# Four of eight token blocks by gathered experts, two of them begun in the front

## The chip, the core and the metric

One core of one Trainium2 chip runs the program. The metric is device time in microseconds (us): the median over runs, lower is better. A core has TensorE (PE, matrix products; its weight loads are listed as PEld), VectorE (DVE), ScalarE (ACT), GpSimd (POOL), SyncE (SP, which here only issues transfers) and 16 DMA engines. Each engine works its instructions off in the order in which the program gives them.

## What is computed

A transformer block on 1,024 tokens of 1,024 channels: latent attention and a gated recurrence side by side, a projection, and then a mixture of 16,384 single-vector experts. The change concerns the mixture:

```
q = (h2 @ w_query) -> 8 heads x 2 halves of 128;  s = q . sub_keys   # 128 scores per half
per head: top 16 of each half, then top 16 of the 256 sums -> 128 experts per token
u = expert_u[idx]; v = expert_v[idx]                                 # 1024 numbers each
act = gelu(h2 . u);  y = sum over 128 experts of softmax(best) * act * v;  x += gate2 * y
```

## The kernel before

The **front** does all up to the experts' choice, in two halves of 512 tokens (part 0, part 1): attention in 32 units, `merge_a`, `lru`, `merge_b`, `ffn_in` (output projection, norm, queries and scores). Matrices there are split into a high and a low fp32r part (`split`, `weight`: ACT casts, DVE subtracts) and multiplied in three products (`lin`, 24 matmuls per 1,024 rows).

The 1,024 tokens are eight blocks of 128. A **dense** block has all 16,384 experts computed and weighted by a table G that holds the chosen ones' weights and zeros elsewhere. A **gathered** block (`GATHER`) has only its chosen 128 rows per token fetched: `gather_u` issues 128 indirect transfers on GpSimd's queue, one expert row for each of the 128 tokens (512 KB), and VectorE multiplies each with h2 and sums it (`g_u`, one reduce); `gather_v` fetches 128 times 512 KB of `expert_v`, and TensorE adds four of them at a time into `g_y`. Before, blocks 0 to 4 are dense and 5 to 7 gathered.

`route` makes the final choice for a block from its top-16 lists; `table` makes G for a dense block in 32 steps, four tokens each: a one-hot row `oneB` (VectorE, one instruction of 512 columns), `oneA` (VectorE, four of 128), four matmuls into `ps_G`, two copies to `gs` on ACT, and now and then a store to `d_G`. These steps, and those of the gathers, wait in a list, `self.steps`, and `pump(n)` takes n of them out at fixed places of the main program, whose order they then share. What is left over after part 1 is taken out in one go (the **tail** of the front).

The **dense stage** runs over 128 groups of 128 experts (i). `first(i)` multiplies the dense tokens with `uT[i]` (`ps_A`, with gelu to `a`); `weigh(i)` multiplies with G and splits (`w`); `second` adds the products with `expert_v` for NGRP groups at once in PSUM (`ps_y`), and VectorE adds that to sums in SBUF (`yac`). After each product of `first` (24 matmuls) and each block of tokens of `second` stands one pump of the gather steps (a point), at a rate that spends them by 91% of these points (`RATE`); only the routes of the gathered blocks go faster, two steps a point. The loads of `uT` and `expert_v` go through two buffers, `raw`, on SP's queue, one serving `uT` and one `expert_v`; the split `v` has NGRP + 1 buffers.

The longest path in the program is set by this written order; nothing is rearranged at run time.

Of the kernel before, what the change touches and what calls it, by code (L numbers as in the profile page):

```python
# [9 lines left out]
F32 = mybir.dt.float32  # L10
# [69 lines left out]
class Builder:  # L80
    def __init__(self, ctx, tc, I, out, dbg=None, stop=None):
# [8 lines left out]
        self.rate = dict(unit=(1, 2), ma=3, lru=6, mb=2, z=4, q=2)  # L90
# [40 lines left out]
    def pump(self, n):  # L131

        for _ in range(min(n, len(self.steps))):
            self.steps.pop(0)()
# [226 lines left out]
    def head(self, p):  # L361
# [67 lines left out]
        def up(u):  # L429

            n = (768, 768, 1024)[u]
            raw = fp.tile([128, n], F32, tag="raw", bufs=3, name="wupraw")
# [53 lines left out]
    def attention(self, p):  # L486
# [7 lines left out]
        vn = self.b8([128, 4, 512], F32, "vn")  # L494
        rq = fp.tile([128, 4, 8], F32, tag="rq", bufs=2, name="rq")
# [40 lines left out]
        def keys(h, blocks):  # L536
            t = heads.setdefault(h, {})
            if 0 in blocks:
# [3 lines left out]
                if p:  # L542
                    nc.sync.dma_start(t["k"][:, 0:512], self.d_k[h])
                    if h % 2 == 0:
                        t["vold"] = fp.tile([128, 4, 128], F32, tag="vold", bufs=2, name="vold")
                        nc.sync.dma_start(t["vold"], self.d_v[:, :, h * 64:h * 64 + 128])
                    else:
                        t["vold"] = heads[h - 1]["vold"]
# [10 lines left out]
        def values(h, i, P):  # L559
# [16 lines left out]
            def mix():  # L576
                for kb in range(n):
                    v = t["vold"][:, kb, :] if kb < p * 4 else vn[:, kb - p * 4, hp * 128:(hp + 1) * 128]
# [96 lines left out]
    def lru(self, p, hs, gb):  # L675
# [7 lines left out]
        def gate(g):  # L683
            t = grp[g] = [fp.tile([128, G, 512], F32, tag="t4", bufs=9, name=nm) for nm in ("ge", "rr", "uu", "bx")]
            for m in range(G):
                wt = self.weight(I["w_in"][8 + g * G + m], 1024)
                ps = self.psum([128, 512], "ps_g")
                self.lin(ps, wt, hs)
                nc.scalar.activation(t[0][:, m, :], ps, AF.Gelu_apprx_tanh)
# [52 lines left out]
        for g in range(8 // G):  # L742
            gate(g)
            for m in range(G):
                conv(g * G + m)
            if g:
                scan(g - 1)
            self.pump(self.rate["lru"])
        for m in range(G):
            gates(8 - G + m)  # L750
            gb(m)
        scan(8 // G - 1)
        self.pump(self.rate["lru"])
# [4 lines left out]
    def merge_a(self, p, hs, attn):  # L758
# [3 lines left out]
        for m in range(8):  # L762
# [9 lines left out]
            self.pump(self.rate["ma"])  # L772
# [15 lines left out]
    def merge_b(self, p, gb, rec, yf):  # L788
        nc, I, fp = self.nc, self.I, self.fp
        for m in range(8):  # L790
# [9 lines left out]
            self.pump(self.rate["mb"])  # L800
# [12 lines left out]
    def ffn_in(self, p, ys):  # L813
# [12 lines left out]
        for cq in range(4):  # L826
# [13 lines left out]
            self.pump(self.rate["z"])  # L840
# [6 lines left out]
        self.normalise(xs, lambda i: fp.tile([128, 1024], F32, tag="raw", bufs=3, name="junk"))  # L847
# [45 lines left out]
        def score(c):  # L893
            qT = qTs.pop(c)
            sk = fp.tile([128, 128], F32, tag="sk", bufs=4, name="sk")
# [9 lines left out]

        late = [i for i in range(4) if p * 4 + i in GATHER]
        for i in range(4):
            if i not in late:
                self.routes[p * 4 + i] = st[:, i], it[:, i]
        soon = [] if 0 in late else self.route(p * 4)[0]  # L910
        self.soon[p * 4] = soon
        for c in range(17):
# [9 lines left out]
            self.pump(self.rate["q"])  # L922
            while len(self.ahead) > max(ahead * (AHEAD - 1 - c) // AHEAD, 0):
                self.ahead.pop(0)()
        if late:
            a, b = late[0], late[-1] + 1
            d = self.d_st[p * 4 + a:p * 4 + b].rearrange("t p k c -> p k t c")
            nc.gpsimd.dma_start(d[:, 0], st[:, a:b].rearrange("p i a b -> p i (a b)"))
            nc.gpsimd.dma_start(d[:, 1], it[:, a:b].rearrange("p i a b -> p i (a b)").bitcast(F32))
# [12 lines left out]
    def route(self, tb):  # L942

        nc = self.nc
        late = tb in GATHER
# [20 lines left out]
        def start():  # L966

            if late:
                sit = self.gv([128, 2, 256], F32, "sit")
                self.after(nc.sync.dma_start(sit, self.d_st[tb]), self.mark)  # L970
# [42 lines left out]
        def pick(w):  # L1013

            eq = new("raw", [128, 128, 16], BF16, "eq", 3)
# [8 lines left out]
        def end():  # L1024
# [6 lines left out]
            if tb in GATHER:  # L1031
                g = self.blocks[tb]
                for n, dt in (("w", F32), ("ei", I32), ("eT", I32)):
                    g[n] = self.gp.tile([128, 128], dt, tag="g_" + n, bufs=3, name="g_" + n)
# [20 lines left out]


    def gather_u(self, g):

        nc, gp, I = self.nc, self.gp, self.I
        us = {}  # L1060

# [350 lines left out]
```

## Time and profile before

| what | value |
|---|---|
| median of 3 runs | 3806.28 us (3798.11 to 3807.5) |
| profiled execution | 3811.1 us, of which the span of the profile is 3809.3 us |
| front, part 1: first unit of attention to last query | 728 to 1640 us |
| front's tail | 1640 to 1720 us |
| dense stage, first matmul to last | 1720 to 3772 us |
| TensorE busy | 3427.5 us, 90% of the span; mean granted clock 0.95 |

A window row of the profile gives, for a stretch of the span, the busy time of each engine (and its instructions), then the clock granted to TensorE as a share of full speed, the mean busy share of the 16 DMA engines, and the GB/s moved. A timeline row gives start, duration, engine, line, operation, what is written and read, a count of merged instructions, and in brackets the idle time before and what ended it.

### The profile page before, as it was taken

Reading aid. Unit: us, or ns where it says so; the run is one execution under the profiler, and the core shown is the slowest. Engines: PE = TensorE matmul, PEld = TensorE weight load, DVE = VectorE, ACT = ScalarE, POOL = GpSimd, SP = SyncE. Lnnn points to the kernel's source line nnn. Section 1 sums busy time; section 2 is a strip of 40 time slices with the busy share of each in tenths; the row PEclk is TensorE's granted clock in tenths of the full one; section 3 lists DMA queues with packets and bytes.
Section 4 is the critical chain, followed back from the end, with each engine's and each line's share of the span. In section 5 each row is a group of like instructions: output and inputs, shape, how many; then the busy total and the mean of one; then the engine's idle time right before and its main releaser. Section 6 shows DMA issues by size and latency. Waiting matters only on the chain. (4 is left out here: it accounts for less than half of the span.)

```text
span 3809.3 us, 50002 instructions
## 1 busy us (share of the span) xinstructions
PE 3427.5 (90%) x18805; PEld 2810.2 (74%) x18805; DVE 2543.8 (67%) x5976; ACT 1271.9 (33%) x2054; POOL 938.1 (25%) x798
## 2 busy tenths in 40 slices
PE   6899989689988966569988999999999999999997
PEld 4577778467876855558977887787788777877786
DVE  5535548986677565588978876677767766744455
ACT  4437443377466332234222222221222222221121
POOL 0000013000000000000144445555555555444400
PEclk8899999799999987779999999999999999999998
DMA  7422443121423331145588899999989999998932
GB/s 306 151 83 90 139 147 119 47 98 42 149 83 119 133 113 54 58 163 151 182 272 276 279 315 326 335 342 342 330 308 335 335 338 324 311 306 310 316 103 92
DMA packets 382521, 792.48 MB, mean 208 GB/s; under 512 B 188660, under 2 KB 209140, under 8 KB 373448
## 3 DMA queue, kind: packets, MB, share of 16 engines
q1 hardware_dynamic: 271464, 385.80, 31.0%
q0 software_dynamic: 110816, 403.49, 29.3%
q8 instruction: 148, 2.42, 0.3%
q14 instruction: 93, 0.76, 0.1%
HBM read 720.23 MB, written 68.96 MB: 207 GB/s over the span
## 5 line engine op out<-in xcount | busy, mean ns | idle before, releaser
L669 PE MATMUL ps_A<-dh,u 128*128 128x320 f32 x2048 | 609.7, 311 | 5.2 <-DVE yac L1267 5.2
L1070 POOL DMA_INDIRECT g_u<-in_expert_u,g_ei x384 | 453.7, 1181 | 620.3 <-DMA raw<-in_uT 218.1
L670 PE MATMUL ps_A<-dh,u 128*128 128x320 f32 x2048 | 605.9, 309 | 0.0
L1076 DVE CUSTOM_DVE_ANT_0 g_u<-g_u,g_h 128x1024 f32<-128x1024 f32 x384 | 465.5, 1222 | 191.8 <-DMA g_u<-in_expert_u,g_ei 190.6
L669 PE MATMUL ps_y<-v,w 128*128 128x512 f32 x1280 | 515.7, 403 | 49.5 <-DVE yac L1267 40.4
L1100 POOL DMA_INDIRECT g_v<-in_expert_v,g_eT x384 | 433.3, 1128 | 459.0 <-PE g_y L1114 131.6
L670 PE MATMUL ps_y<-v,w 128*128 128x512 f32 x1280 | 504.4, 394 | 0.1
L1267 DVE TENSOR_TENSOR yac<-yac,ps_y 128x512 f32<-128x512 f32 x630 | 414.1, 682 | 95.5 <-PE ps_y L672 94.2
L98 ACT CAST v<-raw 128x1024 fp32r<-128x1024 f32 x128 | 134.5, 1050 | 890.1 <-PE ps_y L672 543.4
L669 PEld LDWEIGHTS ps_A<-dh,u 128*128 128x128 f32 x2048 | 385.3, 188 | 38.2 <-issue 20.1
L672 PE MATMUL ps_y<-v,w 128*128 128x512 f32 x1280 | 402.9, 394 | 2.2 <-DVE w L99 0.7
L670 PEld LDWEIGHTS ps_A<-dh,u 128*128 128x128 f32 x2048 | 385.5, 188 | 1.8
L1169 PE MATMUL ps_G<-oneA,oneB 128*128 128x128 f32 x1280 | 226.0, 329 | 160.1 <-DVE oneA L1165 148.3
L669 PEld LDWEIGHTS ps_y<-v,w 128*128 128x128 f32 x1280 | 242.4, 189 | 168.7 <-DVE yac L1267 64.6
L672 PE MATMUL ps_A<-dh,u 128*128 128x320 f32 x2048 | 343.2, 310 | 0.0
L1169 PEld LDWEIGHTS ps_G<-oneA,oneB 128*128 128x128 f32 x1280 | 202.0, 230 | 191.4 <-issue 123.2
L672 PEld LDWEIGHTS ps_A<-dh,u 128*128 128x128 f32 x2048 | 312.4, 189 | 0.0
L99 DVE TENSOR_TENSOR v<-raw,v 128x1024 fp32r<-128x1024 f32 x128 | 156.3, 1221 | 217.5 <-ACT v L98 217.5
L672 PEld LDWEIGHTS ps_y<-v,w 128*128 128x128 f32 x1280 | 242.3, 189 | 62.2 <-DVE w L99 10.0
L670 PEld LDWEIGHTS ps_y<-v,w 128*128 128x128 f32 x1280 | 242.6, 190 | 46.2 <-DVE v L99 0.5
L99 DVE TENSOR_TENSOR whl<-wraw,whl 128x1024 fp32r<-128x1024 f32 (+2 forms) x136 | 155.2, 1145 | 151.1 <-ACT whl L98 151.0
L1172 ACT COPY gs<-ps_G 128x256 f32<-128x256 f32 x320 | 167.6, 641 | 219.5 <-PE ps_G L1169 193.9
(348 smaller groups left out, 5797.2 us busy)
## 6 DMA issues: line engine op xcount, KB each, us to landing
raw<-in_uT SPq DMA_DIRECT2D x128, 512.0 KB
raw<-in_expert_v SPq DMA_DIRECT2D x128, 512.0 KB
d_G<-gs SPq DMA_DIRECT2D x40, 1024.0 KB
Gt<-d_G SPq DMA_DIRECT2D x64, 640.0 KB
wraw<-in_w_in SPq DMA_DIRECT2D x64, 512.0 KB
wada<-in_w_ada SPq DMA_DIRECT2D x32, 512.0 KB
wraw<-in_w_query SPq DMA_DIRECT2D x32, 512.0 KB
x<-in_x SPq DMA_DIRECT2D x16, 512.0 KB
```

Of the source, the lines that this page charges most:

```text
L98: self.nc.scalar.copy(hi, src)
L99: (eng or self.nc.vector).tensor_tensor(lo, src, b32(hi), op=ALU.subtract)
L669: nc.tensor.matmul(ps, lh, rh, start=(n == 0), stop=False)
L670: nc.tensor.matmul(ps, lh, rl, start=False, stop=False)
L672: st = nc.tensor.matmul(ps, ll, rh, start=False, stop=(n == len(terms) - 1))
L1070: st = nc.gpsimd.indirect_dma_start(out=u[:], out_offset=None, in_=I["expert_u"], in_offset=bass.IndirectOffsetOnAxis(ap=g["ei"][:, s:s + ...
L1076: nc.vector.tensor_tensor_reduce(out=u, in0=u, in1=g["h2"], scale=1.0, scalar=0.0, op0=ALU.mult, op1=ALU.add, accum_out=g["act"][:, s:s + 1])
L1100: st = nc.gpsimd.indirect_dma_start(out=v[:], out_offset=None, in_=I["expert_v"], in_offset=bass.IndirectOffsetOnAxis(ap=g["eT"][:, t:t + ...
L1169: nc.tensor.matmul(ps[:, m, :], B[:, m, :], A[:, m, :], start=True, stop=True)
L1172: nc.scalar.copy(t["st"][m][:, :, k:k + 4].rearrange("p i t -> p t i"), ps[:, :, m * 64:(m + 1) * 64])
L1267: nc.vector.tensor_tensor(yac[tb][:, ds], yac[tb][:, ds], ps, op=ALU.add)
```

## The change

Blocks 0, 1, 6 and 7 are gathered, and 2 to 5 dense, so the dense matmuls have 512 tokens and no longer 640. The u rows of blocks 0 and 1 are fetched and reduced in part 1 of the front, through two buffers (`GUF`), between the table steps of blocks 2 and 3; their v rows, and all of blocks 6 and 7, stay in the dense stage. `oneA` goes to GpSimd. `second` adds four groups (NGRP 4, with four `v` buffers, not five), G is stored in pieces of 16 tokens, the front's `raw` has two buffers for three, the top-16 lists of three of each four blocks go through DRAM on SP's queue, and gate2 is loaded for each block at the end.

```diff
-GATHER = (5, 6, 7)
+GATHER = (0, 1, 6, 7)
+SOONER = tuple(b for b in GATHER if b < 4)
+LATER = tuple(b for b in GATHER if b >= 4)
...
-GC = 32
-NGRP = 2
-GU, GV, WB = 4, 8, 3
+GC = 16
+NGRP = 4
+GU, GV, WB = 4, 8, 4
+GUF = 2
...
-        self.rate = dict(unit=(1, 2), ma=3, lru=6, mb=2, z=4, q=2)
+        self.rate = dict(unit=(1, 3.6), w=(1.5, 3.6), z=(4, 8), q=(2, 4))
+        self.credit = 0.0
...
-        raw = self.fp.tile([128, cols], F32, tag="raw", bufs=3, name="wraw")
+        raw = self.fp.tile([128, cols], F32, tag="raw", bufs=2, name="wraw")
...
     def pump(self, n):
 
+        self.credit += n
+        n = int(self.credit + 1e-6)
+        self.credit -= n
...
-            self.pump(self.rate["ma"])
+            self.pump(1.5 * self.rate["w"][p])
...
-        if late:
-            a, b = late[0], late[-1] + 1
-            d = self.d_st[p * 4 + a:p * 4 + b].rearrange("t p k c -> p k t c")
-            nc.gpsimd.dma_start(d[:, 0], st[:, a:b].rearrange("p i a b -> p i (a b)"))
...
+        d = self.d_st[p * 4 + 1:p * 4 + 4].rearrange("t p k c -> p k t c")
+        nc.sync.dma_start(d[:, 0], st[:, 1:4].rearrange("p i a b -> p i (a b)"))
...
+    def after_part(self, p):
+
+        tbs = [tb for tb in range(p * 4, p * 4 + 4) if tb not in LATER]
+        rt = {tb: self.soon.pop(tb) if tb in self.soon else self.routed(tb) for tb in tbs}
+        side = [rt[tb] + self.table(tb) for tb in tbs if tb in DENSE]
+        for tb in tbs:
+            if tb in SOONER:
+                self.steps += rt[tb] + self.merge(self.gather_u(self.blocks[tb]), side.pop(0))
+        self.steps += sum(side, [])
...
+        sooner = g["tb"] in SOONER
+        gp, GUN = (self.fp, GUF) if sooner else (self.gp, GU)
...
-                u = us[s] = gp.tile([128, 1024], F32, tag="gu", bufs=GU, name="g_u")
+                u = us[s] = gp.tile([128, 1024], F32, tag="gu", bufs=GUN, name="g_u")
...
-            s -= GU - 1
+            s -= GUN - 1
...
-        nc.vector.tensor_tensor(gr, y, self.gate2, op=ALU.mult)
+        self.bcast_row(gr, 5)
+        nc.vector.tensor_tensor(gr, y, gr, op=ALU.mult)
...
-                nc.vector.tensor_scalar(A[:, m, :], iota, ch[:, 0, n:n + 1], ch[:, 2, n:n + 1], op0=ALU.is_equal,
+                nc.gpsimd.tensor_scalar(A[:, m, :], iota, ch[:, 0, n:n + 1], ch[:, 2, n:n + 1], op0=ALU.is_equal,
...
-        points = (128 * 2 + len(groups) * NB) * RATE
+        points = (128 * -(-TD // 512) + len(groups) * NB) * RATE
...
-                Vs[i] = load(I["expert_v"][i * 128:(i + 1) * 128, :], da, "v", NGRP + 1)
+                Vs[i] = load(I["expert_v"][i * 128:(i + 1) * 128, :], da, "v", NGRP)
...
-            us = [self.gather_u(self.blocks[tb]) for tb in GATHER]
+            us = [self.gather_u(self.blocks[tb]) for tb in LATER]
             vs = [self.gather_v(self.blocks[tb]) for tb in GATHER]
-            for b in range(len(GATHER) + 1):
-                self.steps += self.merge(us[b] if b < len(GATHER) else [], vs[b - 1] if b else idle * IDLE[1])
+            for n, v in enumerate(vs):
+                self.steps += self.merge(us[n] if n < len(us) else [], v)
```

Where instructions move is seen on three engines. First VectorE in `merge_a` of part 1, where `whl` is the low part of a weight that TensorE waits for, and `yf` the gated product; before:

```order
L771 TENSOR_TENSOR yf<-ps_pa,sg 128x512
L1165 TENSOR_SCALAR oneA<-cst,ch 128x128
L1161 TENSOR_TENSOR oneB<-cst,ch 128x512
L1165 TENSOR_SCALAR oneA<-cst,ch 128x128 x4
L99 TENSOR_TENSOR whl<-wraw,whl 128x1024
L99 TENSOR_TENSOR whl<-wraw,whl 128x512
```

The same place with the change (g_u is a reduce over a fetched row, g_act the read-out of its sum):

```order
L777 TENSOR_TENSOR yf<-ps_pa,sg 128x512
L103 TENSOR_TENSOR whl<-wraw,whl 128x1024
L103 TENSOR_TENSOR whl<-wraw,whl 128x512
L1102 ISA g_u,g_act<-g_u,g_h_6060 128x1024
L1102 ISA g_act 128x1
L1102 ISA g_u,g_act<-g_u,g_h_6060 128x1024
L1102 ISA g_act 128x1
L1189 TENSOR_TENSOR oneB<-cst,ch 128x512 x2
```

So reduces that wait for a transfer now stand between the weight splits, and the `oneA` rows are gone from this queue. Counted over the whole order, the 256 reduces of part 1 stand 69 in the attention units, 35 in `merge_a`, 45 in `lru`, 35 in `merge_b`, 32 in `ffn_in` ahead of the queries and 40 among the queries. Of the one-hot steps, 126 stood in part 1 and 34 in the tail; with the change 64 and 64.

Second GpSimd's queue in part 1. Before, it held two stores of the top-16 lists between part 0 and the dense stage:

```order
L347 TENSOR_TENSOR hT<-nfull,hT 128x512 x2
L99 TENSOR_TENSOR whl<-wraw,whl 128x1024 x12
L928 DMA d_st<-st 128x3x256
L929 DMA d_st<-it 128x3x256
L1070 DMA g_u<-in_expert_u,g_ei 128x1024 x128
```

With the change (a piece of it):

```order
L1193 TENSOR_SCALAR oneA<-cst,ch 128x128 x4
L1096 DMA g_u<-in_expert_u,g_ei 128x1024 x2
L1193 TENSOR_SCALAR oneA<-cst,ch 128x128
L1096 DMA g_u<-in_expert_u,g_ei 128x1024
L1193 TENSOR_SCALAR oneA<-cst,ch 128x128 x7
L1096 DMA g_u<-in_expert_u,g_ei 128x1024 x4
```

Gather issues now share a queue with the one-hot rows. Third TensorE in the dense stage, at the step from `first` to `second`; before:

```order
L672 MATMUL ps_A<-dh_13393,u 128x320 x4
L1114 MATMUL g_y<-g_v,g_z 32x512 x8
L669 MATMUL ps_y<-v,w 128x512
L670 MATMUL ps_y<-v,w 128x512
L669 MATMUL ps_y<-v,w 128x512
L670 MATMUL ps_y<-v,w 128x512
L672 MATMUL ps_y<-v,w 128x512 x2
```

With the change:

```order
L677 MATMUL ps_A<-dh_13875,u 128x512 x4
L677 MATMUL ps_A<-dh_13884,u 128x512 x4
L1141 MATMUL g_y<-g_v,g_z 32x512 x8
L674 MATMUL ps_y<-v,w 128x512
L675 MATMUL ps_y<-v,w 128x512
...
L675 MATMUL ps_y<-v,w 128x512
L677 MATMUL ps_y<-v,w 128x512 x4
```

All dense matmuls now have 512 columns, and a sum in `ps_y` takes 12 of them, over four groups of experts, before VectorE adds it.

## Rows read from the trace of the kernel before

**Rows 1.** Windows of the dense stage; the columns are explained above.

```profile
1720.00:1865.00 145.00, 144.82 (x827) 132.36 (x826) 131.93 (x375) 55.74 (x78) 0.42 (x1) 1.00 0.49 147
1865.00:2250.00 385.00, 349.24 (x1869) 309.24 (x1868) 314.89 (x481) 86.07 (x121) 179.30 (x144) 0.97 0.84 276
2250.00:3315.00 1065.00, 1043.55 (x6068) 841.68 (x6067) 751.85 (x1122) 226.04 (x322) 576.55 (x497) 1.00 0.95 333
3315.00:3625.00 310.00, 310.00 (x1876) 233.10 (x1878) 138.96 (x183) 63.42 (x91) 130.71 (x128) 1.00 0.88 300
3625.00:3772.00 147.00, 147.00 (x841) 134.16 (x834) 75.60 (x93) 35.39 (x51) 0.00 (x0) 1.00 0.31 90
```

**Rows 2.** Windows of 100 us of the dense stage: the one with most GB/s.

```profile
2420.00:2520.00 100.00, 99.66 (x590) 79.72 (x589) 72.71 (x111) 22.32 (x31) 58.65 (x50) 1.00 0.97 344
```

**Rows 3.** Windows of the front's part 1 by stage, and its tail.

```profile
728.00:950.00 222.00, 190.58 (x1167) 146.82 (x1166) 165.65 (x615) 155.75 (x332) 0.00 (x0) 0.93 0.21 75
950.00:1047.00 97.00, 94.37 (x520) 80.85 (x520) 60.49 (x158) 46.20 (x78) 0.00 (x0) 1.00 0.41 146
1047.00:1210.00 163.00, 135.77 (x586) 107.29 (x585) 121.20 (x271) 110.74 (x145) 0.00 (x0) 0.91 0.28 93
1210.00:1302.00 92.00, 92.00 (x468) 78.61 (x468) 57.69 (x118) 39.76 (x63) 0.00 (x0) 0.99 0.41 138
1302.00:1380.00 78.00, 64.25 (x468) 60.97 (x468) 51.08 (x90) 24.63 (x35) 0.00 (x0) 0.91 0.42 142
1380.00:1640.00 260.00, 162.88 (x697) 139.85 (x696) 145.48 (x701) 58.92 (x101) 0.00 (x0) 0.79 0.16 56
1640.00:1720.00 80.00, 47.21 (x290) 40.69 (x288) 76.30 (x252) 38.31 (x76) 1.75 (x2) 0.82 0.49 194
```

**Rows 4.** Timeline of PE in the dense stage, two places: starts of matmuls.

```profile
3377.08 1.92 PE L1114 MATMUL g_y<-g_v,g_z 128*32 128x512 f32 x16
3378.94 0.42 PE L669 MATMUL ps_A<-dh,u 128*128 128x320 f32 x1
...
3643.09 0.39 PE L669 MATMUL ps_y<-v,w 128*128 128x512 f32 x1
3644.45 0.39 PE L669 MATMUL ps_y<-v,w 128*128 128x512 f32 x1
3653.97 0.30 PE L669 MATMUL ps_A<-dh,u 128*128 128x320 f32 x1
3657.49 0.31 PE L669 MATMUL ps_A<-dh,u 128*128 128x320 f32 x1
```

**Rows 5.** Timeline, the first gathers and their reduces, transfers still few.

```profile
1864.58 1.01 POOL L1070 DMA_INDIRECT g_u<-in_expert_u,g_ei  x1 [215.53 <-DMA raw<-in_uT]
1867.93 0.97 POOL L1070 DMA_INDIRECT g_u<-in_expert_u,g_ei  x1 [2.34 <-PE ps_y L672]
1868.80 1.23 DVE L1076 CUSTOM_DVE_ANT_0 g_u<-g_u,g_h 128x1024 f32<-128x1024 f32 x1 [0.93 <-DMA g_u<-in_expert_u,g_ei]
1872.60 1.23 DVE L1076 CUSTOM_DVE_ANT_0 g_u<-g_u,g_h 128x1024 f32<-128x1024 f32 x1 [1.43 <-DMA g_u<-in_expert_u,g_ei]
```

**Rows 6.** The tile g_u over the whole span: its transfers.

```profile
DMA to landing us min/median/max: 4.2/7.2/12.1
```

**Rows 7.** Groups by line: oneA on VectorE, and GpSimd's subtractions.

```profile
L1165 DVE TENSOR_SCALAR oneA<-cst,ch 128x128 f32<-128x128 f32 x640 | 182.1, 338 | 0.0
L99 POOL TENSOR_TENSOR whl<-wraw,whl 128x1024 fp32r<-128x1024 f32 x16 | 39.1, 2452 | 70.4 <-ACT whl L98 58.9 <-DMA kT<-d_k 11.5
L347 POOL TENSOR_TENSOR hT<-nfull,hT 128x512 fp32r<-128x512 f32 x8 | 10.2, 1284 | 554.2 <-ACT hT L346 554.0
```

**Rows 8.** Timeline, one load of expert_v: transfer, cast, subtraction.

```profile
2621.80 0.33 SPq L1216 DMA_DIRECT2D raw<-in_expert_v  x1
2626.18 1.05 ACT L98 CAST v<-raw 128x1024 fp32r<-128x1024 f32 x1 [4.71 <-DMA raw<-in_expert_v]
2627.26 1.23 DVE L99 TENSOR_TENSOR v<-raw,v 128x1024 fp32r<-128x1024 f32 x1 [1.81 <-ACT v L98]
```

More of the change, by code (lines that the diff above doesn't have):

```diff
@@ L745, in lru @@
                 conv(g * G + m)
+                self.pump(self.rate["w"][p])
             if g:
                 scan(g - 1)
-            self.pump(self.rate["lru"])
         for m in range(G):
@@ L751, in lru @@
             gb(m)
+            self.pump(self.rate["w"][p])
         scan(8 // G - 1)
-        self.pump(self.rate["lru"])
         if p == 1:
@@ L904, in score @@
                 self.top16(sc[:, i, :], w2, st[:, i, c, :], it[:, i, c, :])
[L906 to L911, printed above, removed]
+        self.routes[p * 4] = st[:, 0], it[:, 0]
+        soon = self.soon[p * 4] = self.routed(p * 4)
         for c in range(17):
@@ L944, in route @@
         nc = self.nc
-        late = tb in GATHER
+        late = tb in LATER
         t = {}
@@ L966, in start @@
         def start():
-            if late:
-                sit = self.gv([128, 2, 256], F32, "sit")
-                self.after(nc.sync.dma_start(sit, self.d_st[tb]), self.mark)
+            if tb not in self.routes:
+                sit = new("sit", [128, 2, 256], F32, "sit")
+                dma = nc.sync.dma_start(sit, self.d_st[tb])
+                if late:
+                    self.after(dma, self.mark)
                 st, it = sit[:, 0, :].rearrange("p (a b) -> p a b", b=16), \
@@ L1032, in end @@
                 g = self.blocks[tb]
-                for n, dt in (("w", F32), ("ei", I32), ("eT", I32)):
-                    g[n] = self.gp.tile([128, 128], dt, tag="g_" + n, bufs=3, name="g_" + n)
+                for n, dt in (("w", F32), ("ei", I32)):
+                    g[n] = (self.gp if late else self.fp).tile([128, 128], dt, tag="g_" + n, bufs=2 if late else 1, name="g_" + n)
+                g["eT"] = self.kept(g, [128, 128], I32, "eT")
                 nc.vector.tensor_copy(g["w"], W2)
@@ L1083, in end @@
             nc.tensor.transpose(pt, g["act"], self.ident)
-            g["wT"] = gp.tile([128, 4, 32], F32, tag="g_wT", bufs=2, name="g_wT")
+            g["wT"] = self.kept(g, [128, 4, 32], F32, "wT")
             nc.vector.tensor_copy(g["wT"], pt.rearrange("p (a b) -> p a b", a=4))
-            g["y"] = self.pg.tile([128, 1024], F32, name="g_y")
-        return [start] + [lambda s=s: step(s) for s in range(128 + GU - 1)] + [end]
+        return [start] + [lambda s=s: step(s) for s in range(128 + GUN - 1)] + [end]
     def gather_v(self, g):
@@ L1095, in step @@
         def step(n):
+            if n == 0:
+                g["y"] = self.pg.tile([128, 1024], F32, name="g_y")
             if n < 128:
@@ L1117, in step @@
                                          start=(r == 0), stop=(r == 31), tile_position=(0, q * 32))
-        return [lambda n=n: step(n) for n in range(128 + GV - 4)] + [lambda: self.finish(gp, g["tb"], g["y"], "gv", GV)]
+        return [lambda n=n: step(n) for n in range(128 + GV - 4)] + [lambda: self.finish(gp, g["tb"], g.pop("y"), "gv", GV)]
     @staticmethod
@@ L1333, in run @@
                     continue
-                for tb in range(p * 4, p * 4 + 4):
-                    if tb in DENSE:
-                        self.steps += (self.soon[tb] if tb in self.soon else self.route(tb)[0]) + self.table(tb)
+                self.after_part(p)
             self.pump(1 << 30)
@@ L1342, in run @@
               tc.tile_pool(name="psd", bufs=6, space=bass.MemoryType.PSUM, reuse_waits="tile") as self.ps):
-            turns, idle = [], [lambda: None]
-            self.steps += idle * IDLE[2]
-            for tb in GATHER:
+            idle = [lambda: None]
+            turns = []
+            for tb in LATER:
                 st, turn = self.route(tb)
-                self.steps += [f for g in st[:4] + turns + st[4:] for f in [g] + idle]
+                self.steps += st[:4] + turns + st[4:]
                 turns = [turn]
```

39 lines of the change are left out of this document (21 added, 18 removed).

## The prediction

> **What bounds the kernel now.** I read the windows of the dense stage first, because the change takes a fifth of its columns away. From 1720 to 3772 us TensorE is busy nearly all the time: 1043.55 of 1065 us in the middle, 310 of 310 in the next stretch, 147 of 147 in the last [rows 1]. It is the bound there. But the second column to look at is the DMA share: 0.95 with 333 GB/s in the middle, and the best 100 us anywhere move 344 GB/s at a share of 0.97 [rows 1, 2]. So the transfers stand right behind TensorE, and a saving on TensorE is worth only what the transfers let through. Then the windows of part 1 of the front: TensorE is full in `merge_a` (94.37 of 97 us) and `merge_b` (92 of 92); in the units VectorE is busy for 165.65 of 222 us, in the queries neither is full, and the granted clock is 0.79, so for some of the time at the lower of its two levels [rows 3]. VectorE has about 310 us free in the 912 us from 728 to 1640 (601.6 us busy over the six rows), and the DMA share is 0.16 to 0.42. That is room for transfers, but scattered room on VectorE.
>
> **Dense stage, TensorE.** A dense matmul of 320 columns takes 3.52 us for 24, so 0.1467 us; six of 512 columns take 1.36 us, so 0.2267 us each [rows 4]. A batch of sixteen `g_y` moves the next matmul by 2.0 us (1.86 from start to start, and a little at the next) [rows 4]. Before: 6144 of 320, 3840 of 512 and 96 batches: 901 + 871 + 192 = 1964 us, near the 2052 measured. With the change: 6144 of 512 and 128 batches: 1393 + 256 = 1649 us, 315 us less.
>
> **Dense stage, transfers.** Gathers in this stage stay 768 of 0.524 MB (256 of u, 512 of v). The stage has 256 points of 24 matmuls (5.44 us each). The two routes take 34 steps, 17 points. The other 798 steps go over 216 points, 3.7 a point; 23 points remain. In the first 144 points u and v are fetched together: 512 gathers, 268.4 MB, and 144/256 of the 167.8 MB of `uT`, `expert_v` and G, together 362.8 MB. At 344 GB/s that is 1055 us; TensorE needs 144 x 5.44 + 64 x 2.0 = 911. The transfers win. In the next 72 points (v alone) 181.4 MB need 527 us and TensorE 520. So:
> routes 17 x 5.44 = 93, both kinds 1055, v alone 527, the last 23 points 125, the finish 37 as before (3772 to 3809). That is 1837. Two queues that nearly fill each other's slots lose something: in the middle stretch before, 21 of 1065 us (2%) [rows 1]. I take 2.7% of the 1582, 43 us: 1880 us. Before it was 3809 - 1720 = 2089. **Gain 209 us**; bounds 115 (at 325 GB/s, between the 333 of the middle stretch and the 300 of the next [rows 1], with the same loss) and 290 (at a share of 1.0, 344/0.97 = 355 GB/s, and no loss). The Trainium skill (SBUF — State Buffer, section "A bandwidth-pool intuition that's wrong (but worth ruling out)") gives about 358 GB/s from HBM to one core; by it the two stretches would need 1013 and 507 us and the sum would be 62 us lower. No window of this trace reaches that.
>
> **Part 1, the gathers.** 256 gathers come in. With two buffers, gather s can be issued only when reduce s-2 has ended. From issue to reduce start the first ones took 4.2 and 4.7 us, with few transfers about, the reduce 1.23 [rows 5]; with some 0.3 us from a reduce's end to the next issue, a buffer's round is about 6 us and two buffers give one gather per 3.0 us. Against the counts of the order: units 69 x 3.0 = 207 us in 222; `merge_a` 105 in 97, 8 over; `lru` 135 in 163; `merge_b` 105 in 92, 13 over; `ffn_in` 96 in 78, 18 over; queries 120 in 260 [rows 3]. That is 39 us where the stage is too short for its gathers; behind a reduce that waits stand weight splits, and TensorE waits for those. VectorE's own work: 256 x 1.23 = 315 us come, and of one-hot steps 501 `oneA` at 182.1/640 = 0.285 us of busy time (143 us) and half of the `oneB` go. It grows by some 130 us. Most falls into idle time; I take a third, 43. What TensorE saves on 62 table steps there I take as nothing, it is in the same waits. **Loss 82**, rounded to 80. Bounds: 0 (all in the 310 us free), and 330: by the median landing of 7.2 us [rows 6] a gather takes 4.35 us, which is 287 us over, and the 43.
>
> GpSimd's `oneA` stands in the same queue as the gather issues; it has no row. Its subtractions took 1.284 us for 512 columns and 2.452 for 1024 [rows 7], 2.28 ns a column, so 0.41 us for 128 on that line. VectorE takes 0.338 [rows 7]. Bounds: VectorE's and the 1.284 us of the shortest GpSimd row. I take 0.41, by the line.
>
> **The tail.** Before, 34 table steps stand there, bound by VectorE (76.30 of 80 us busy [rows 3]): about 62 us of steps. Now two tables, 64 steps, at 4 x 0.41 = 1.64 us: 105 us, 43 more. A second route comes too, through a store and a load of its lists, some 20 us on VectorE, partly beside the first table: 22 with its waits. **Loss 65.** Bounds: 20 (TensorE and ACT alone set the step) and 290 (1.284 us a row).
>
> **Part 0 and the rest.** Two blocks' h2 rows are now made in part 0: five VectorE instructions of 1024 columns, 6 us, and two stores on SP that hold its queue until the last top-16: **8 us**. Two `raw` buffers for three in the front cost nothing while a load (4.4 us from issue to cast [rows 8]) is shorter than the 5.4 us of its 24 matmuls; if VectorE's split comes late, that cover is gone, and each late load costs the difference. The gate2 rows at the end of a block hide behind the other gathers.
>
> **Sum** against the profiled execution: 3811 + 8 + 80 + 65 - 209 = 3755. It lay 5 us above the median of the runs shown, so 3750.
>
> **Rivals.**
> *Slower, by the two buffers.* In the loaded stage a gather took 7.2 us to land, not 4.2 [rows 6]. If it is 6.3 in the front, with GpSimd's one-hot rows ahead of the issue counted in, a gather takes 3.9 us: 47 us over in the units, 40 in `merge_a`, 13 in `lru`, 45 in `merge_b`, 47 in `ffn_in`, 192 in all, with the 43 of VectorE 235. Time: 3811 + 8 + 235 + 65 - 209 = 3910, median 3905. It decides from about 3.4 us a gather on. For it: reduces wait in an ordered queue. Against: the DMA share of part 1 is a third of the loaded one [rows 3]. Chance 0.16.
> *Much faster.* The reduces fall into VectorE's free time as they were spread for that, and the one-hot rows cost no more than on VectorE: 15 in part 1, 40 in the tail, and 235 gained in the dense stage: 3811 + 8 + 15 + 40 - 235 = 3639, median 3635. For it: 310 us are free [rows 3]. Against: TensorE is already full in two stages whose order now holds 35 waits each. Chance 0.2.
> *The sums of four wait for expert_v.* With four `v` buffers the first of a group can be cast only after the last matmul of the sum before; three more come through the one `raw` buffer, 6.7 us each from issue to the end of the split [rows 8]. 2.3 + 3 x 6.7 = 22.4 us, in a gap of four `first` (21.8 us) and a `g_y` batch or two. If VectorE is 3 us late each time, TensorE waits 5 us in each of 32 groups; less what the transfers would have cost anyway, 130 us are lost: 3885, median 3880. It decides from 8 us a load on. Chance 0.08.
> *GpSimd held up by VectorE.* GpSimd's 16 subtractions vary about a mean of 2.452 us against twice 1.284 [rows 7], which shows no great hold-up so far. If a one-hot row is held for half a reduce or half an `oneB`, it takes 0.7 to 1.0 us: tail +130, part 1 +110: 3850, median 3845. The Trainium skill says as much (SBUF — State Buffer, section "Who interferes with whom"): a VectorE instruction with two inputs in SBUF contends with a GpSimd instruction that reads SBUF, and the second to start waits. Both kinds stand side by side here. Chance 0.06.
>
> **Numbers.** The forecast has 0.5, with a range of its own of 3690 to 3800. A difference of 0.3% (11 us) is about what a measurement of this kernel can tell from none. Of the forecast's 0.5, 0.44 lie below 3795, 0.05 within, 0.01 above. Faster 0.64, same 0.05, slower 0.31. The range of 3620 to 3900 leaves out half of the first two rivals.
>
> **What would show it.** Right: dense stage of about 1880 us with a DMA share of 0.95 or more while u and v are fetched, and TensorE busy for some 85 to 90% there; part 1 longer by about 80 us, most of it in `merge_a`, `merge_b` and `ffn_in`, with VectorE waiting for g_u; `oneA` on GpSimd at 0.4 us; a tail of about 145 us. Wrong: a gather period above 3.4 us in part 1 and TensorE behind VectorE; `oneA` at 0.7 us or more; matmuls of `ps_y` waiting for `v`; or a dense stage whose DMA share falls below 0.9 while TensorE is not full.

## The result and the profile after

The changed kernel takes **3989.89 us** (3968.51 to 4002.31, four runs) against 3806.81 us for the kernel before in the same session: the ratio is **1.0481, 95% interval 1.0424 to 1.0537**, so it is slower by 4.8%. The forecast was 3750 us and faster. The profiled execution took 4002.31 us, with a span of 4000.5.

The windows of part 1 by stage (units, `merge_a`, `lru`, `merge_b`, `ffn_in`, queries), then of the tail; the columns are those of [rows 3]:

```profile
737.00:965.00 228.00, 188.26 (x899) 136.43 (x899) 161.77 (x497) 122.84 (x263) 112.03 (x104) 0.79 0.59 186
965.00:1125.00 160.00, 118.25 (x471) 91.15 (x470) 78.20 (x144) 39.20 (x66) 110.24 (x100) 0.82 0.56 181
1125.00:1370.00 245.00, 147.43 (x542) 108.79 (x542) 151.63 (x282) 103.14 (x128) 88.12 (x74) 0.76 0.52 169
1370.00:1512.00 142.00, 89.88 (x373) 72.49 (x373) 93.34 (x149) 30.48 (x43) 72.30 (x57) 0.80 0.61 200
1512.00:1640.00 128.00, 87.02 (x475) 75.10 (x475) 72.54 (x136) 29.49 (x47) 73.91 (x68) 0.72 0.61 194
1640.00:1882.00 242.00, 152.33 (x649) 124.04 (x648) 174.73 (x728) 53.00 (x87) 123.92 (x113) 0.80 0.50 161
1882.00:2117.00 235.00, 201.58 (x519) 129.36 (x520) 89.29 (x189) 66.55 (x130) 217.40 (x256) 0.50 0.27 99
```

Part 1 takes 1145 us, before 912; the tail takes 235, before 80 [rows 3]. In the tail the last engine column, GpSimd, is busy for 217.40 of 235 us: it is the bound there. In part 1 no engine is full in any stage: every one waits for another. The dense stage is as forecast; its windows answer to [rows 1]:

```profile
2117.00:2221.00 104.00, 98.05 (x415) 79.75 (x415) 80.19 (x236) 42.12 (x56) 0.00 (x0) 0.95 0.53 147
2221.00:3300.00 1079.00, 957.73 (x4430) 683.79 (x4429) 652.70 (x977) 226.06 (x288) 583.66 (x512) 0.96 0.95 339
3300.00:3856.00 556.00, 548.03 (x2804) 356.13 (x2802) 196.18 (x261) 115.26 (x148) 264.33 (x256) 1.00 0.95 334
```

From 2117 us to the end are 1883.5 us (forecast 1880, before 2089). While u and v are fetched together, the DMA share is 0.95 and TensorE is busy for 89%.

So the loss is in the front. `oneA` on GpSimd, first in the page's groups over the whole span, then in the groups of the tail; busy time and mean ns stand behind the bar:

```profile
L1193 POOL TENSOR_SCALAR oneA<-cst,ch 128x128 f32<-128x128 f32 x512 | 494.5, 976 | 37.6 <-DVE rU L934 30.1
```

```profile
L1193 POOL TENSOR_SCALAR oneA<-cst,ch 128x128 f32<-128x128 f32 x256 | 217.4, 863 | 33.7 <-DVE rU L934 30.1 <-ACT ch L1180 3.6
```

A row takes 0.86 us in the tail and 0.98 over all; VectorE took 0.338 [rows 7]. The waits of part 1 (who waits for what, us in total, times, longest):

```profile
DVE g_u L1102 <- DMA g_u<-in_expert_u,g_ei: 342.5, 156, 9.1
POOL g_u L1096 <- DVE g_act L1102: 331.4, 125, 10.9
...
PE ps_G L1197 <- POOL oneA L1193: 126.0, 91, 13.5
...
PE ps_G L1197 <- DVE oneB L1189: 69.9, 12, 13.5
...
PE ps_gw L1109 <- DVE g_act L1107: 51.2, 1, 51.2
```

VectorE waits 342.5 us for rows, GpSimd 331.4 us for reduces that would free a buffer: each for the other, through a transfer. TensorE's queue is ordered too: it stands still where the one-hot rows of a table step are late (`ps_G`, 126.0 and 69.9 us), and once for the end of a block's gathers (`ps_gw`). One place in `merge_a`, GpSimd's timeline and then VectorE's:

```profile
1048.13 0.95 POOL L1096 DMA_INDIRECT g_u<-in_expert_u,g_ei  x1 [0.30 <-issue]
1049.11 9.28 POOL L1193 TENSOR_SCALAR oneA<-cst,ch 128x128 f32<-128x128 f32 x8
1058.56 1.03 POOL L1096 DMA_INDIRECT g_u<-in_expert_u,g_ei  x1 [0.17 <-issue]
...
1051.29 1.23 DVE L1102 CUSTOM_DVE_ANT_0 g_u<-g_u,g_h 128x1024 f32<-128x1024 f32 x1 [3.14 <-DMA g_u<-in_expert_u,g_ei]
1053.47 1.23 DVE L1102 CUSTOM_DVE_ANT_0 g_u<-g_u,g_h 128x1024 f32<-128x1024 f32 x1 [0.95 <-DMA g_u<-in_expert_u,g_ei]
```

The reduce that ends at 1052.5 frees a buffer, but the next gather is issued only at 1058.56: eight `oneA` rows hold GpSimd's queue for 9.28 us.

### The profile page after: what moved, and what is told of

Same layout as the page of the kernel before. It is cut to its first block, busy times and chain, and to the rows that moved or that the text cites. A ratio compares the mean times of both kernels' runs of the same rounds, so it can differ in the third digit from the quotient of the medians.

```text
span 4000.5 us, 43166 instructions
## 1 busy us (share of the span) xinstructions
PE 3347.2 (84%) x15220; PEld 2453.5 (61%) x15220; DVE 2265.5 (57%) x5212; ACT 1192.7 (30%) x1860; POOL 1697.7 (42%) x1564
## 4 chain that ended last, share of the span: by engine, by line
PE 28%; DMA 23%; issue 16%; DVE 15%; POOL 14%; ACT 4%; SPq 0%; POOLq 0%; DVEq 0%; ACTq 0%
DMA raw<-in_uT 11%; POOL oneA L1193 9%; DMA g_u<-in_expert_u,g_ei 7%; POOL g_u L1096 5%; DMA raw<-in_expert_v 3%; DVE g_u L1102 3%; PE ps_y L674 3%; PE g_y L1141 2%; PE ps_y L677 2%; PE ps_y L675 2%; PE ps_A L674 2%; PE ps_A L675 2%; PE ps_A L677 2%; ACT u L102 1%; PE ps_s L633 1%
## 5 line engine op out<-in xcount | busy, mean ns | idle before, releaser
L1102 DVE CUSTOM_DVE_ANT_0 g_u<-g_u,g_h 128x1024 f32<-128x1024 f32 x512 | 623.6, 1226 | 433.1 <-DMA g_u<-in_expert_u,g_ei 420.7
L1197 PE MATMUL ps_G<-oneA,oneB 128*128 128x128 f32 x1024 | 342.3, 449 | 239.1 <-POOL oneA L1193 144.5
L1193 POOL TENSOR_SCALAR oneA<-cst,ch 128x128 f32<-128x128 f32 x512 | 494.5, 976 | 37.6 <-DVE rU L934 30.1
L674 PE MATMUL ps_A<-dh,u 128*128 128x512 f32 x1024 | 424.4, 414 | 69.6 <-ACT u L102 64.0
L674 PE MATMUL ps_y<-v,w 128*128 128x512 f32 x1024 | 416.5, 407 | 63.2 <-DVE yac L1294 39.7
L675 PE MATMUL ps_A<-dh,u 128*128 128x512 f32 x1024 | 414.0, 404 | 0.0
L1127 POOL DMA_INDIRECT g_v<-in_expert_v,eT x256 | 288.9, 1128 | 279.1 <-DVE yac L1294 104.8
L103 DVE TENSOR_TENSOR u<-raw,u 128x1024 fp32r<-128x1024 f32 x128 | 156.7, 1224 | 442.4 <-ACT u L102 409.7
L675 PE MATMUL ps_y<-v,w 128*128 128x512 f32 x1024 | 405.9, 396 | 0.0
L1127 POOL DMA_INDIRECT g_v<-in_expert_v,g_eT x256 | 264.3, 1033 | 289.4 <-PE g_y L1141 185.6
L674 PEld LDWEIGHTS ps_A<-dh,u 128*128 128x128 f32 x1024 | 201.2, 197 | 171.4 <-ACT u L102 85.4
L674 PEld LDWEIGHTS ps_y<-v,w 128*128 128x128 f32 x1024 | 195.6, 191 | 167.9 <-issue 51.1
L677 PE MATMUL ps_y<-v,w 128*128 128x512 f32 x1024 | 282.2, 397 | 0.0
L1141 PE MATMUL g_y<-g_v,g_z 128*32 128x512 f32 x2048 | 255.8, 599 | 1.5 <-DMA g_v<-in_expert_v,g_eT 1.5
L677 PE MATMUL ps_A<-dh,u 128*128 128x512 f32 x1024 | 253.1, 389 | 0.9 <-DVE u L103 0.9
```

What stands on the lines that cost most here:

```text
L103: (eng or self.nc.vector).tensor_tensor(lo, src, b32(hi), op=ALU.subtract)
L674: nc.tensor.matmul(ps, lh, rh, start=(n == 0), stop=False)
L675: nc.tensor.matmul(ps, lh, rl, start=False, stop=False)
L677: st = nc.tensor.matmul(ps, ll, rh, start=False, stop=(n == len(terms) - 1))
L1102: nc.vector.tensor_tensor_reduce(out=u, in0=u, in1=g["h2"], scale=1.0, scalar=0.0, op0=ALU.mult, op1=ALU.add, accum_out=g["act"][:, s:s + 1])
L1127: st = nc.gpsimd.indirect_dma_start(out=v[:], out_offset=None, in_=I["expert_v"], in_offset=bass.IndirectOffsetOnAxis(ap=g["eT"][:, t:t + ...
```

## The experiments

Theory 1: GpSimd's `oneA` is the loss, in the tail as the bound and in part 1 by holding the queue of the gather issues. Theory 2: the chain of gathers over two buffers is the loss of part 1.

To compare many kernels, stages are marked in one way: part 1 runs from the start of the first `PT` (a tile of part 1's first attention unit) to that of the last instruction on `sc` (the scores), the tail from there to the first `ps_A`, the dense stage from there to the end. So marked, part 1 and tail of the change have 1132 and 240 us (1145 and 235 in the windows above), before 898 and 74. The expectation of the first run uses the windows, later ones these marks. Times are medians in us; the ratio is to the kernel before on the same chip (3800 to 3811 us there); stages are those of one profiled execution.

| kernel | part 1 | tail | dense | time | ratio to before (95%) |
|---|---|---|---|---|---|
| before | 898 | 74 | 2089 | 3806 | |
| the change | 1132 | 240 | 1884 | 3990 | 1.0481 (1.0424–1.0537) |
| oneA on VectorE, 2 buffers | 1082 | 146 | 1881 | 3844 | 1.0091 (1.0057–1.0124) |
| oneA on VectorE, 3 buffers | 987 | 146 | 1858 | 3755 | 0.9867 (0.9837–0.9898) |
| oneA on GpSimd in the tail only, 2 buffers | 1084 | 240 | 1857 | 3932 | 1.0317 (1.0278–1.0355) |
| before, oneA on GpSimd | 911 | 127 | 2086 | 3869 | 1.0169 (1.0130–1.0209) |
| oneA on GpSimd, 3 buffers | 1045 | 239 | 1849 | 3902 | 1.0286 (1.0229–1.0343) |
| 3 buffers, one row of four on GpSimd in the tail | 989 | 135 | 1861 | 3743 | 0.9858 (0.9823–0.9893) |
| 3 buffers, sums of two, G by two | 995 | 146 | 1928 | 3827 | 1.0084 (1.0054–1.0113) |
| 3 buffers, half reduces | 946 | 146 | 1878 | 3722 (1 run) | |
| 3 buffers, sums of two, G by four | 983 | 146 | 1891 | 3781 | 0.9957 (0.9927–0.9987) |
| 3 buffers, half of uT | 989 | 146 | 1789 | 3676 (1 run) | |
| 3 buffers, spread rates | 973 | 149 | 1885 | 3740 | 0.9822 (0.9802–0.9842) |
| 3 buffers, spread rates, one row on GpSimd | 972 | 135 | 1874 | 3734 | 0.9825 (0.9789–0.9861) |

The dense stage of one and the same code lies between 1848 and 1885 us in these profiles; smaller differences there tell nothing. Part 1 lies between 983 and 995 us in the five versions of three buffers whose edit stands behind it. "3 buffers" in the lower rows means with oneA on VectorE.

**oneA on VectorE again.**

```diff
-                nc.gpsimd.tensor_scalar(A[:, m, :], iota, ...
+                nc.vector.tensor_scalar(A[:, m, :], iota, ...
```

> The changed kernel with one edit undone: the weighted one-hot rows (oneA) are made on VectorE again; everything else stays. Theory 1 (GpSimd's rows are the loss: 0.79 us and more each instead of 0.41, they bound the tail, and in part 1 they hold GpSimd's queue so that gathers are issued late): the tail falls from 235 us to about 157 (64 steps at 1.83 us of VectorE plus 40), part 1 (1145 us from its first unit to the tail) falls by 60 to 114 (64 steps that held the queue for at least 3.1 us each, against 1.35 us of VectorE each that come back), the time is 3800 to 3850 us. Theory 2 (the chain of gathers over two buffers is the loss of part 1, whatever stands in GpSimd's queue): only the tail falls, part 1 stays or grows by up to 40 us, the time is 3910 to 3950 us.

3843.92 us: 146 us less than the change. Windows of its part 1 and its tail:

```profile
755.00:1837.00 1082.00, 724.96 (x3370) 582.62 (x3369) 780.24 (x2138) 376.50 (x619) 290.81 (x253) 0.82 0.57 185
1837.00:1982.00 145.00, 81.16 (x524) 69.54 (x525) 143.05 (x475) 65.11 (x134) 0.00 (x0) 0.84 0.42 160
```

The tail falls by 94 us and is now full on VectorE (143.05 of 145). Part 1 falls by 50, a little less than Theory 1 asked. What is left of part 1's loss, 184 us over the kernel before, Theory 1 does not explain.

**And a third buffer.**

```diff
-GUF = 2
+GUF = 3
-              tc.tile_pool(name="front_a", bufs=9, reuse_waits="tile") as fa,
+              tc.tile_pool(name="front_a", bufs=7, reuse_waits="tile") as fa,
```

> As the kernel with oneA on VectorE again, and a third buffer for the front's gathered rows (its 4 KB come from seven instead of nine buffers of the tag t2). Theory 1: with GpSimd's queue free, two buffers were enough; within 20 us of the kernel with oneA on VectorE. Theory 2: the third buffer takes the landing time out of the chain (VectorE waited about 343 us for rows in part 1), and part 1 is shorter by 100 us or more than in the kernel with oneA on VectorE and two buffers.

The buffers of `t2` hold `PT`, `oneB` and others. With the third buffer the program also places each reduce one step later behind the issue of its gather, so the buffer and this order change together.

3755.43 us, below the kernel before. The window of its part 1, and below it VectorE's largest wait there:

```profile
750.00:1737.00 987.00, 706.71 (x3371) 571.01 (x3369) 772.37 (x2135) 376.09 (x619) 308.48 (x252) 0.84 0.61 203
```

```profile
DVE g_u L1102 <- DMA g_u<-in_expert_u,g_ei: 123.6, 79, 6.7
```

The wait for rows is 123.6 us (246.1 with two buffers) and part 1 is 95 us shorter, a little less than the 100 that Theory 2 asked: it holds for that much. Both theories are right, for different parts.

**GpSimd in the tail only.** `oneA` by `(nc.vector if tb < 4 else nc.gpsimd)`, two buffers.

> oneA on VectorE for the two token blocks whose tables are made in part 1, on GpSimd for the two of the tail. Theory 1: part 1 is as in the kernel with oneA on VectorE throughout (60 to 114 us shorter than in the changed kernel), the tail stays at about 235 us; 3880 to 3930 us. Theory 2: part 1 stays or grows by up to 40 us, the tail stays: 3990 to 4030 us.

3931.98 us, 2 above the range of Theory 1: the tail is the change's (240), part 1 that of VectorE's rows (1084). The two parts of oneA's price are thus separate.

**The one edit on the kernel before.** There `nc.vector.tensor_scalar` becomes `nc.gpsimd.tensor_scalar`, no more.

> The kernel before with this one edit alone: oneA on GpSimd, no gathers in the front. Theory 1: the tail becomes bound by GpSimd, 34 steps of 4 rows at 0.86 us are 117 us, with 18 of other work 135 instead of 80 us; part 1 gains at most what VectorE is relieved of where it was waited for (126 steps of 1.35 us, 170 us busy, a half of them at most on the path): 3775 to 3860 us. Theory 2: GpSimd's rows are hidden, the tail is at most 25 us longer, the time no more than 3806 us.

3869.40 us, slower by 1.7%: the tail grows by 53 us, and part 1 by 13, although VectorE has 116 us less to do in it (473.73 us busy instead of 590.18). That is 9 us above the range of Theory 1, which had given part 1 a gain. No stage is shorter by more than 3 us.

**oneA on GpSimd with three buffers.** The change with `GUF = 3` and seven buffers of `t2`.

> The changed kernel with a third buffer for the front's gathered rows (seven instead of nine of t2), oneA on GpSimd as in the change. So far oneA on GpSimd costs part 1 some 50 us and the second buffer's lack some 95, and the tail 94. If the two add up: part 1 is 95 us shorter than in the changed kernel, about 1036 us, the tail stays at 240, the time is about 3895 us. If the third buffer covers the time that oneA holds GpSimd's queue: part 1 is 987 us or less, as with oneA on VectorE, the time is about 3845 us. If the queue is what holds the gathers whatever the buffers: under 40 us gained, 3950 us or more.

3901.93 us, part 1 of 1045: the two prices add. Part 1 is 87 or 95 us shorter by the third buffer, and 50 or 58 by VectorE's rows, in either order. By the medians the third buffer is worth 88 us both times, and VectorE's rows in part 1 are worth 58 (from the change to GpSimd in the tail only). Seven buffers of `t2` for nine were not tried alone.

**One of four rows on GpSimd, in the tail.** `(nc.gpsimd if tb > 3 and m == 0 else nc.vector)`, on the version of three buffers.

> The kernel with oneA on VectorE and three buffers, but of the four rows of a step in the tail one is made by GpSimd. VectorE's part of a step falls from 1.83 to 1.49 us, GpSimd's is 0.86 us and hidden: 64 steps save 22 us, the tail is about 125 us instead of 146, the time about 3735 us. Rival: VectorE and GpSimd slow one another when they run side by side, or PE's lower clock takes the gain: tail within 8 us of 146.

The tail falls by 11 us, half of the expected 22; the time, 3742.61 us, cannot be told from 3755. The tile `oneA` in its tail (duration in ns: least, median, most):

```profile
L1193 DVE TENSOR_SCALAR oneA<-cst,ch x196: 326/364/430, 1749.1 to 1877.1; 128x128 f32<-128x128 f32 x196
L1193 POOL TENSOR_SCALAR oneA<-cst,ch x64: 1191/1384/1390, 1767.1 to 1876.0; 128x128 f32<-128x128 f32 x64
```

GpSimd's row takes 1.38 us here, where VectorE is never idle between the rows; in the change's tail, where VectorE mostly waits, the median was 0.79. VectorE's timeline in the tail, first with all rows on VectorE (the version of three buffers), then in this run:

```profile
1757.35 0.69 DVE L1189 TENSOR_TENSOR oneB<-cst,ch 128x512 f32<-128x512 f32 x1
1757.95 1.11 DVE L1193 TENSOR_SCALAR oneA<-cst,ch 128x128 f32<-128x128 f32 x4
1758.97 0.69 DVE L1189 TENSOR_TENSOR oneB<-cst,ch 128x512 f32<-128x512 f32 x1
```

```profile
1799.96 0.71 DVE L1189 TENSOR_TENSOR oneB<-cst,ch 128x512 f32<-128x512 f32 x1
1800.56 0.94 DVE L1193 TENSOR_SCALAR oneA<-cst,ch 128x128 f32<-128x128 f32 x3
1801.33 0.71 DVE L1189 TENSOR_TENSOR oneB<-cst,ch 128x512 f32<-128x512 f32 x1
```

VectorE's instructions follow one another without a gap in both, so VectorE alone accounts for the step: 1.63 us there, 1.37 here. (GpSimd's rows follow without a gap too: both are full.) The difference is one row from start to start, 0.26 us; the expectation had taken a row's duration, 0.34, but durations overlap. So 64 steps save 17 us, not 22. Most of the 6 that are then still missing are lost behind the last step, where the first dense matmul waits for copies of G, and they for a store; with all rows on VectorE it did not wait:

```profile
1882.77 2.37 ACT L1200 COPY gs<-ps_G 128x256 f32<-128x256 f32 x5 [3.73 <-DMA d_G<-gs]
1883.40 0.79 PE L674 MATMUL ps_A<-dh,u 128*128 128x512 f32 x1 [4.75 <-ACT gs L1200]
```

**Sums of two.** `NGRP = 2`, on the version of three buffers.

> The kernel with oneA on VectorE and three buffers, with sums of two expert blocks instead of four in the dense stage (and so two buffers of v). If the dense stage goes by its transfers, as forecast, the time stays within 15 us of 3755 us. If the sums of four are what shortened it (half the additions to yac, 84 us of VectorE less), the dense stage is 40 us or more longer than 1858 us.

The dense stage is 70 us longer. But not only the additions changed: the packets of the stage, for the version of three buffers and for this one:

```profile
DMA packets 283175, 586.03 MB, mean 316 GB/s; under 512 B 148416, under 2 KB 148416, under 8 KB 283072
```

```profile
DMA packets 414955, 586.71 MB, mean 304 GB/s; under 512 B 280032, under 2 KB 280032, under 8 KB 414850
```

The bytes are the same, the small packets nearly twice as many: G for two blocks comes in pieces half as long. So a further run parts the two.

**Sums of two, G by four.** `factors` fetches four blocks' G at a time, and `v` has four buffers.

> As the kernel with oneA on VectorE and three buffers, with sums of two expert blocks, but the factors G fetched for four blocks at a time and four buffers of v, as in the sums of four. The kernel with sums of two and G by two had a dense stage of 1928 us instead of 1858, 504 additions to yac for 248, and 280,032 packets under 512 B in it for 148,416. If the smaller packets of G were its loss: the dense stage is within 20 us of 1858 us. If the additions on VectorE were: it stays above 1900 us.

3780.95 us, a dense stage of 1891, 33 us over 1858 and between the two expectations. That is only 6 us over the longest profile of the unchanged stage; the ratios, whose intervals do not touch, put it at 0.9%, some 34 us. So the sums of four are worth some 30 us: `yac` has 504 additions of 0.682 us for 248, and TensorE waits 75.3 us for `w` at `ps_y` where it waited 20.7. But its wait for the cast of `u` fell from 74.7 to 6.9 us, so one wait largely took the place of the other, and how the additions make the stage longer is not shown. The other 37 of the 70 us are the small packets or the two `v` buffers, which stays open.

**Half reduces.** The reduce reads 512 of the 1024 columns.

```diff
+                m = 512 if sooner else 1024
-                nc.vector.tensor_tensor_reduce(out=u, in0=u, in1=g["h2"], ...
+                nc.vector.tensor_tensor_reduce(out=u[:, :m], in0=u[:, :m], in1=g["h2"][:, :m], ...
```

> The kernel with oneA on VectorE and three buffers, where the front's reductions read 512 of the 1024 columns of a gathered row (the gathers are whole; the products of the other half are left out). If what is left of part 1's loss (some 89 us over the kernel before) is VectorE's own work for the gathers, 256 reductions shorter by about 0.55 us take 140 us off VectorE, and part 1 falls from 987 us by 60 us or more. If the transfers' landing is the bound, VectorE waits that much longer for rows, and part 1 falls by less than 30 us.

One execution. Part 1 falls by 41 us, between the two expectations. VectorE is busy for 641.25 us instead of 772.37, and waits longer for rows:

```profile
DVE g_u L1103 <- DMA g_u<-in_expert_u,g_ei: 191.8, 108, 8.1
```

Of 131 us taken off VectorE, 68 came back as waiting for transfers. So what is left of the loss is in part VectorE's work, and the landing time takes up half of what is saved on it.

**Half of uT.** `us[i + 1] = load(...) if i % 2 else us[i]`.

> The kernel with oneA on VectorE and three buffers, where every second block of uT is not loaded but the one before it is used again (64 loads of 512 KB, with their casts and splits, are left out). If the dense stage goes by its transfers, 33.5 MB less at 342 GB/s take up to 98 us off it until PE's own 1724 us of work bound it: 1760 to 1790 us instead of 1858. If PE or VectorE sets it, it stays within 25 us.

One execution; with the loads their casts on ACT and splits on VectorE are left out too. The dense stage takes 1789 us, 69 less. In its longest window TensorE is busy for 1023.75 of 1080 us, and the transfers are still at their rate:

```profile
1985.00:3065.00 1080.00, 1023.75 (x4865) 735.48 (x4864) 649.17 (x986) 208.66 (x277) 618.02 (x548) 0.97 0.96 345
```

TensorE's wait for the cast of `u` in the dense stage, in the version of three buffers and in this one:

```profile
PE ps_A L674 <- ACT u L102: 74.7, 33, 8.5
```

```profile
PE ps_A L674 <- ACT u L102: 7.8, 1, 7.8
```

ACT's cast itself waited for the load, 462.2 us in the longest window of the version of three buffers and 92.6 us here, so it was the loads and not the casts or splits that held TensorE. With fewer bytes to fetch the gathers go through sooner. The transfers thus hold the stage; as far as this run goes they are worth 69 us of it. Without them another wait grows: that for `w` at `ps_y`, from 20.7 to 54.4 us.

**Spread rates.** `rate=dict(unit=(1, 3), w=(1.5, 3), z=(4, 7), q=(2, 7))`, on the version of three buffers.

> As the kernel with oneA on VectorE and three buffers, with part 1's rates of side steps lower ahead of the queries (3 for 3.6, 7 for 8) and higher in them (7 for 4), so that gathers which now end in the middle of the queries are spread to their end, where VectorE waited 66 us for scores. If VectorE's load in the stages ahead is what makes part 1 long, it falls from 987 us by 25 to 50 us, and the time is 3705 to 3730 us. If the gathers only wait elsewhere: within 12 us of 3755 us, or more where steps are left for the tail.

3740.12 us; part 1 is 14 us shorter, about half of the least expected, and 10 us under the shortest of the unchanged part 1.

**Both small edits.**

> The two small edits together on the kernel with oneA on VectorE and three buffers: the spread rates (part 1 shorter by 14 us in their own run) and one of four rows of the tail by GpSimd (tail shorter by 11 us in its own run). If the two are independent: about 3730 us, ratio to the kernel before 0.980. If they are only scatter of one execution: 3745 to 3760 us.

3733.79 us, ratio 0.9825 (0.9789 to 0.9861): as expected of two independent edits, and the fastest version by its median. But its ratio is that of the spread rates alone (0.9822), and its interval overlaps those of all versions with three buffers, VectorE's rows and sums of four. Against the change it saves 256 us.

## Why the prediction was wrong

**Dense stage: right.** 1883.5 us for 1880; that the two agree within 4 us is partly luck, as the stage varies by 37 us from profile to profile. Its stretches came out at 104 us (routes, forecast 93), 1079 (both kinds, 1055 and the loss of 2.7%: 1083), 556 (v alone, 541) and 144.5 (the rest, 162). That transfers win there is shown by the run with half of uT. The ceiling of 344 GB/s held over the long stretch (339), not in each 100 us: from 2600 to 2700 us the change moved 373. (The prediction's sentence on a higher rate should say 49 us, not 62, as its own 520 us of TensorE bound the second stretch.) The sum costed the sums of four at nothing on VectorE; they are worth some 30 us, which the forecast did not need, because it did not name a stage without them. No wait for `v` appears among TensorE's larger ones; that rival is out.

**Tail: the price of `oneA` was mis-sized.** The term was 65, by 0.41 us a row; the row costs 0.86 and the tail grew by 155 to 166. The 0.41 came from a line through two GpSimd rows of another operation, at 512 and 1024 columns, prolonged to 128. The upper end, 1.284 us, held the true value; the price that I took lay close to the lower, VectorE's. Why the row alone takes 0.79 us and not 0.41, by a fixed part or by its two scalars per partition, no run shows. With VectorE's rows a step takes 1.63 us, as the 1.64 that I had, and the tail grows by 72, so the rest of that term (64 steps, a second route) was about right.

**Part 1: the step that failed is "a gather per 3.0 us" against the length of each stage.** The 3.0 itself is right where nothing else runs. The change's timeline of VectorE at the end of block 0's gathers, first and last of nine reduces (TensorE stands still here, in its wait at `ps_gw`):

```profile
1221.30 1.22 DVE L1102 CUSTOM_DVE_ANT_0 g_u<-g_u,g_h 128x1024 f32<-128x1024 f32 x1 [0.94 <-DMA g_u<-in_expert_u,g_ei]
...
1245.76 1.23 DVE L1102 CUSTOM_DVE_ANT_0 g_u<-g_u,g_h 128x1024 f32<-128x1024 f32 x1 [1.79 <-DMA g_u<-in_expert_u,g_ei]
```

These are eight rounds in 24.46 us, 3.06 each. But I compared rounds with stage lengths as if VectorE's other work ran inside them. It stands in the same ordered queue: while VectorE waits for a row it does nothing else, and while it does something else the reduce that frees a buffer is late. In `merge_a` 35 gathers took 160 us, 4.6 each; over the 1132 us of part 1 it was 4.4 each. Of the loss of 233 us, the runs assign some 90 to the second buffer's lack (87 and 95), some 55 to `oneA` on GpSimd (50 and 58), and 89 remain with neither. There VectorE is busy for 772.37 and waits for rows for 123.6 of 987 us; before it was busy for 590.18 of 898. My "a third of 130 us" stood for this, at 43. The 130 came true in the change (732 us of VectorE in the six rows above, against 602), and a third is also what the half reduces gave: 41 us of part 1 for 131 us of VectorE. At that rate the 182 us that VectorE has more to do in the version of three buffers would be 57 of the 89, an estimate; the other 32 stay open.

TensorE did not wait only for the weight splits that I had named. It waited 54.6 us for weights in part 1 of the change (2.5 before), and 196 us for one-hot rows of the table steps, which I had left at nothing as part of the same waits. The wait for rows of `oneA`, before and in the version of three buffers:

```profile
PE ps_G L1169 <- DVE oneA L1165: 128.5, 48, 8.4
```

```profile
PE ps_G L1197 <- DVE oneA L1193: 177.5, 43, 10.2
```

The table steps are half as many there, and TensorE waits longer for them. The wait of 51.2 us at `ps_gw` I had not named either; it is 5.9 us with VectorE's rows and two buffers, and gone with three buffers.

Two things no run parts from the rest. The front's `raw` at two buffers I took at nothing as long as loads come in time: ACT waited 3.8 us for the loads of weights in part 1 before, 56.8 in the change and 79.8 with three buffers and VectorE's rows. And TensorE's clock: the mean granted was 0.90 in part 1 before, 0.79 in the change and 0.84 with three buffers, so for more of the time at the lower of its two levels, while TensorE was idle for 167, 359 and 280 us. The some 2,870 matmuls other than `ps_G` kept it busy for 550, 633 and 600 us. How much of this stood on the path is open.

**Part 0.** The 8 us do not show: part 1 starts at 745.0 us in the change and at 748.2 before (747 to 760 in the other versions with gathers in the front).

**The rivals.** "Slower, by the two buffers" had the place right, at 3905; "GpSimd held up by VectorE" had nearly the right price of a row, at 3845. They were weighed as if one excluded the other. Both came, in different stages, and their losses add: part 1 of the first (235) with the tail of the second (130) gives 3970 us, 20 below the measured time. The hold-up itself is only part of that price: the median of 0.79 us where VectorE mostly waits is GpSimd's own; in part 1 the mean was 1.08 and the longest row 6.40. The rule named there (the Trainium skill, SBUF — State Buffer, section "Who interferes with whom") lets either of the two wait for the other. The trace agrees for GpSimd, with 1.38 us beside a busy VectorE; VectorE's `oneB` and rows came as closely behind one another as without GpSimd's row (0.60 and 0.26 us from start to start).

The 4.2 us from issue to landing held for the first gathers; over part 1, with oneA on VectorE and two buffers, the median was 4.9.

## What to carry to other kernels

Work that waits for a transfer in an ordered queue is not hidden by that engine's free time: count its waits as busy, and give it one more buffer than the bare round needs; here a third buffer of 4 KB per partition, with the reduces one step later, was worth 2.3%. Before an operation is moved to an engine that has no row for it, take the bound, not a line through another operation, and look at what else stands in the new engine's queue (here the issues of the gathers). Rivals that sit in different stages should be added, not only weighed. Price a row in a full queue from start to start, not by its duration.

## What the runs showed of the hardware

- A GpSimd `TENSOR_SCALAR` over 128x128 f32 with two scalars per partition took 0.78 to 0.79 us at best, 2.3 times VectorE's 0.34, and 1.38 us in the steady run beside a VectorE that never idled, while VectorE lost nothing from start to start (a row's recorded duration went from 0.336 to 0.364 us). In that run VectorE's `oneB` (two operands, 0.71 us with its overlap) and three rows (0.94) alternated; which of them holds GpSimd was not tried apart.
- In the tails fed by GpSimd, of the change and of the kernel before with the one edit, the granted clock was 0.50, the lower of TensorE's two levels (1.2 of 2.4 GHz), and the median `ps_G` matmul took 0.42 us; TensorE's weight loads waited there for each of GpSimd's rows (in the change 256 times, 93.8 us in all). Fed by VectorE, in the version with two buffers, the mean clock was 0.84 and the median matmul 0.275 us.
